# Set points for the side jobs of the scan, two operand buffers, and placed weight loads and stores

## The chip, the cores and the metric

The kernel runs on one core of a Trainium2 chip. The metric is the device time of one execution in microseconds (us); of several runs the median is taken. TensorE is called PE (its weight loads PEld), VectorE DVE, ScalarE ACT, GpSimd POOL. SP is the engine that issues nearly all DMAs here, one after the other.

## The reference

One step of a bidirectional diffusion backbone in fp32: 128 context and 1024 latent tokens of width 1024 go through SwiGLU FFN, token mixer, SwiGLU FFN, each between two RMS norms with modulation. The change is in the mixer:

```python
r, k, v, g, cb, cc, xc, gate_a, gate_b = split(h @ w_in)          # 5632 columns, 44 blocks of 128
kk = k * k_k; kk = kk * rsqrt(sum(kk * kk) + 1e-12)               # 8 heads of 64
for d in (forward, backward):
    decay = exp(-exp(w_log(xw)));  a = sigmoid(lora(xa));  k_d = k * (1 + (a - 1) * k_a)
    # per token: S = S * w + (S @ -kk) (kk * a)^T + v k_d^T ;  y = S @ r
    y_d, s_d = rwkv7_scan(r, decay, k_d, v, kk, a, s0[d], reverse=(d == 1))
y = groupnorm(y_0 + y_1) + bonus * v;  y_a = (y * sigmoid(g)) @ w_branch_a
y_b = (cb * conv3(cc * xc)) @ w_branch_b
out = (sigmoid(gate_a) * y_a + sigmoid(gate_b) * y_b) @ w_out
```

Latents start from a given state, the context from zero; the final context states are returned too.

## The kernel before

Activations lie transposed, 128 channels by tokens, the 1152 tokens in three tiles of 384. A product with a weight block is made of three matmuls for each 128 rows (high and low parts of fp32); `load_w` brings the weights (`wst`, two transfers of 256 KB for a column block), ACT rounds them to `whi` and POOL takes the rest as `wlo`. In the mixer each of the 44 column blocks of `w_in` is such a dense projection, `proj`: 24 triples, 72 matmuls into `pj`, evacuated by ACT to `fso` and stored to DRAM.

The scan works in chunks of 64 tokens, 18 items: 8 for each of two groups of heads (`g`), then 2 for the context. An item is a front for either direction (`stage_b`: load `ops` from DRAM, form decays, the products `scr`, the transposed operand `bkt`), a triangular solve on DVE (`solve`, its matmuls `l` and `l64b`), and two `step`s that carry the state (`sq`, `yp`). These make the chain. Three kinds of side jobs prepare and finish it: `stage_k` normalises k over heads (loads `or`, `ok`, `od`, `oi`; matmuls `cps`, `kkb`, `bon`; stores kk and the bonus `bvd`), `stage_v` transposes v, `finish` applies group norm and gate (`ysq`, `gv`) and stores `yad`. The rest of `proj` is filler, a generator (`stream`) of triples; `fill(40)` follows each item, and `need` fills on until a job that the chain waits for is written down.

What sets the order: a scheduler lists each engine's instructions by priority (chain 40000, side jobs 39000, filler least) and by its own idea of when an operand is ready; on the chip each engine then goes through its list in that order. A side job runs in a `Lane`: it yields a number of triples to wait between its steps, and its matmuls are put behind the filler triple that stands last (`PB.anchor`). Before the change the first projections (`job_rkv(1)`) are written ahead of the scan, the first four `stage_k` and those of item 0 as a whole without an anchor, weights are loaded as far ahead as three `wst` buffers let them, and every store is issued where its evacuation is written.

```python
        def fill(n):
            for _ in range(n):
                PB.anchor = next(filler, PB.anchor)
                clock["now"] += 1
                if clock["now"] - clock["side"] >= SG_ and any(lanes[x].tick() for x in "fkv"):
                    clock["side"] = clock["now"]
```

After the scan the two branches are read back (`brl`), split, and multiplied (`pb`, `pa`). What is left of the filler is run between.

## Time and profile before

| | us |
|---|---|
| median of 3 runs | 3284.18 (3278.63 to 3292.68) |
| profiled execution: device time, span of its instructions | 3273.45, 3271.7 |
| PE busy in it | 2994.4 (92%) |
| DVE, ACT, POOL busy | 1882.2, 1186.8, 394.7 |
| from the last product of the low-rank stage to the first `pb` | 1061.8 to 2190.4 |

How to read it: a row of the chain or the timeline has its start, its length and its name; what stands in brackets is the idle time of that engine just before it and what ended it. Engine, line and tile name an instruction (`PE cps L168`); two tiles with an arrow are what is written and what is read. PEclk is the share of the full TensorE clock, 2.4 GHz, that was granted; it has two levels, full and half.

### The profile page before, as it was taken

The numbers are of one execution on the slowest core, as the hardware profiler recorded it, in microseconds if no ns is written. First come the engines' busy times: TensorE is split into PE (matmuls) and PEld (weight loads), VectorE is DVE, ScalarE is ACT, GpSimd is POOL, SyncE is SP. The second block draws the span as 40 slices with busy tenths as digits, with TensorE's granted clock in tenths as the row PEclk, the third lists the DMA queues.
The fourth block names the chain that finished last, engine by engine and source line by source line (L and its number), as shares of the span: only waits on it lengthen the run. The fifth ranks groups of instructions, "written<-read, shape, count | busy, mean of one in ns | idle before, by whom it ended". The sixth has DMA issues, their size and how long they took to land.

```text
span 3271.7 us, 53390 instructions
## 1 busy us (share of the span) xinstructions
PE 2994.4 (92%) x20636; PEld 2816.4 (86%) x20636; DVE 1882.2 (58%) x4231; ACT 1186.8 (36%) x2726; POOL 394.7 (12%) x327
## 2 busy tenths in 40 slices
PE   8999999999989677787878888999989999999998
PEld 5999999999988565666767777799989999999998
DVE  7535665565872254677768889646683233323366
ACT  5521111114546242454445555332554211121244
POOL 1000000001250110122222222100130000000012
PEclk9999999999989787888889899999989999999999
DMA  8423333325544332322223332245532111111244
GB/s 270 145 62 96 97 103 86 88 83 154 160 123 163 101 100 65 107 74 88 71 63 98 101 93 84 86 153 158 170 103 84 39 44 45 43 40 42 81 145 132
DMA packets 470761, 330.67 MB, mean 101 GB/s; under 512 B 27424, under 2 KB 448620, under 8 KB 470508
## 3 DMA queue, kind: packets, MB, share of 16 engines
q1 hardware_dynamic: 469880, 326.78, 33.1%
q8 instruction: 162, 2.65, 0.3%
q14 instruction: 91, 0.75, 0.1%
q10 hardware_dynamic: 308, 0.44, 0.0%
q0 software_dynamic: 320, 0.04, 0.0%
HBM read 265.58 MB, written 61.60 MB: 100 GB/s over the span
## 4 chain that ended last, share of the span: by engine, by line
PE 40%; DVE 12%; DMA 8%; issue 4%; ACT 2%; SPq 1%; POOL 0%; DVEq 0%; ACTq 0%; POOLq 0%
PE po L211 3%; PE po L210 3%; PE po L212 3%; PE pg L212 3%; PE pg L211 3%; PE pg L210 3%; PE pu L210 3%; PE pu L212 3%; PE pu L211 3%; DMA oi<-opd 2%; PE pj L705 2%; PE pj L706 2%; PE pj L707 2%; DVE un L1031 2%; DMA opd<-oi 2%
## 5 line engine op out<-in xcount | busy, mean ns | idle before, releaser
L138 ACT ACTIVATE whi<-wst 128x512 fp32r<-128x512 f32 (+1 forms) x578 | 352.9, 612 | 771.2 <-PE po L212 391.5
L139 DVE TENSOR_TENSOR wlo<-wst,whi 128x512 fp32r<-128x512 f32 (+1 forms) x480 | 326.1, 680 | 314.2 <-ACT whi L138 304.2
L705 PE MATMUL pj<-hh,wlo 128*128 128x384 f32 x1056 | 390.1, 370 | 2.3 <-ACT fso L716 1.3
L706 PE MATMUL pj<-hl,whi 128*128 128x384 f32 x1056 | 389.1, 368 | 2.3 <-DVE hl L265 1.3
L707 PE MATMUL pj<-hh,whi 128*128 128x384 f32 x1056 | 387.4, 367 | 0.0
L211 PE MATMUL pg<-hl,whi 128*128 128x384 f32 x1056 | 356.4, 338 | 5.9 <-POOL hl L263 4.6
L210 PE MATMUL pg<-hh,wlo 128*128 128x384 f32 x1056 | 357.3, 338 | 1.3 <-DVE wlo L139 1.3
L210 PE MATMUL po<-ah,wlo 128*128 128x384 f32 x1056 | 354.8, 337 | 2.4 <-ACT ah L138 2.4
L212 PE MATMUL pg<-hh,whi 128*128 128x384 f32 x1056 | 355.5, 337 | 0.0
L210 PE MATMUL pu<-hh,wlo 128*128 128x384 f32 x1056 | 355.0, 336 | 0.0
L211 PE MATMUL po<-al,whi 128*128 128x384 f32 x1056 | 354.2, 336 | 0.4 <-DVE al L139 0.4
L211 PE MATMUL pu<-hl,whi 128*128 128x384 f32 x1056 | 354.0, 335 | 0.0
L212 PE MATMUL pu<-hh,whi 128*128 128x384 f32 x1056 | 353.8, 335 | 0.0
L212 PE MATMUL po<-ah,whi 128*128 128x384 f32 x1056 | 353.6, 335 | 0.0
L273 POOL TENSOR_TENSOR ss<-ss,sqt 128x384 f32<-128x384 f32 x78 | 89.3, 1148 | 1663.7 <-ACT sqt L272 1659.1
L426 DVE TENSOR_TENSOR sil<-sil,pu 128x384 f32<-128x384 f32 x132 | 72.8, 552 | 353.3 <-PE pu L212 353.3
L398 DVE TENSOR_TENSOR o<-o,po 128x384 f32<-128x384 f32 x288 | 159.1, 552 | 166.2 <-PE po L212 165.4
L706 PEld LDWEIGHTS pj<-hl,whi 128*128 128x128 f32 x1056 | 214.2, 203 | 11.3 <-DVE hl L265 2.1
L705 PEld LDWEIGHTS pj<-hh,wlo 128*128 128x128 f32 x1056 | 214.2, 203 | 11.1 <-issue 3.6
L707 PEld LDWEIGHTS pj<-hh,whi 128*128 128x128 f32 x1056 | 213.9, 203 | 8.1 <-issue 3.1
L211 PEld LDWEIGHTS pg<-hl,whi 128*128 128x128 f32 x1056 | 200.1, 190 | 8.4 <-POOL hl L263 6.2
L139 POOL TENSOR_TENSOR wlo<-wst,whi 128x512 fp32r<-128x512 f32 x98 | 134.1, 1372 | 594.5 <-ACT whi L138 459.5
(586 smaller groups left out, 5743.0 us busy)
## 6 DMA issues: line engine op xcount, KB each, us to landing
wst<-in_ffn_w SPq DMA_DIRECT2D x324, 256.0 KB
wmod<-in_w_mod SPq DMA_DIRECT2D x144, 256.0 KB
ops<-opd SPq DMA_DIRECT2D x36, 768.0 KB
wst<-in_w_in SPq DMA_DIRECT2D x94, 256.0 KB
wst<-in_ffn_w SPq DMA_DIRECT2D x96, 192.0 KB
xo<-xd SPq DMA_DIRECT2D x64, 192.0 KB
wst<-in_w_out SPq DMA_DIRECT2D x48, 256.0 KB
opd<-zv SPq DMA_DIRECT2D x24, 384.0 KB
```

The lines of the kernel that those rows point to most:

```text
L138: S.activation(out=hi, in_=src, func=AF.Copy)
L139: eng.tensor_tensor(out=lo, in0=src, in1=hi.bitcast(F32), op=ALU.subtract)
L210: PE.matmul(ps, lo, xh, start=(k == 0), stop=False)
L211: PE.matmul(ps, hi, xl, start=False, stop=False)
L212: later.tick(PE.matmul(ps, hi, xh, start=False, stop=(k == nk - 1)))
L273: eng.tensor_tensor(out=ssum, in0=ssum, in1=q, op=ALU.add)
L398: V.tensor_tensor(out=O[m][t], in0=O[m][t], in1=ps, op=ALU.add)
L426: V.tensor_tensor(out=s, in0=s, in1=pu, op=ALU.mult)
L705: PE.matmul(ps, lo, xh, start=(k == 0), stop=False)
L706: PE.matmul(ps, hi, xl, start=False, stop=False)
L707: ins = PE.matmul(ps, hi, xh, start=False, stop=(k == 7))
L1031: V.tensor_tensor(out=pv, in0=a, in1=b, op=ALU.mult)
```

## The change

- The first projections of heads 2 and 3 (`job_rkv(1)`) become part of the filler, which so grows from 38 to 41 column blocks. The first four `stage_k` and two `stage_v` calls become lane jobs ahead of item 0, with filler until they are done; those of item 0 become lane jobs too.
- A lane job's first instruction of a step, a load or an ACT or DVE operation, is also tied behind the filler triple (`first`), and the gaps grow: from the loads to the first operation 6 to 16 triples (now yielded ahead of the arithmetic), from norm to broadcast 6 to 14, in `finish` 3 to 6; between two steps of any job at least 2 triples, after each `stage_k` 8. The bonus comes last in `stage_k`, and the squares have a buffer of their own (`oa`).
- Weights of a projection are loaded behind the first triple of the one before (`plan`, `fetch`); a store is issued at the first triple that comes at least 6 after its evacuation (`late`, `stores`).
- `ops` has two buffers of five planes instead of one of six; the decay plane goes by two transfers of its own, in pieces of 256 bytes, into one of two `sg` tiles, and its scaling moves to the low-rank stage. `bk` is formed in place, so its transposition takes 8 matmuls of 64 rows instead of 4 of 128.
- Smaller scratch: `cent` has 64 columns, the widest product of the solve is made in two halves.

```diff
-    def load_w(src, nk, eng=V):
+    def load_w(src, nk, eng=V, behind=None):
...
+                dma = SP.dma_start(st[:, :n], src[k0 * 128:(k0 + n) * 128].rearrange("(k p) m -> p k m", p=128))
+                if behind is not None:
+                    after(dma, behind)
...
+        def first(self, ins):
+            self.put(ins)
...
-    cent = small("cent", 128)
-    V.scalar_tensor_tensor(out=cent, in0=bones, scalar=-1.0 / 64, in1=ident, op0=ALU.mult, op1=ALU.add)
+    cent = small("cent", 64)
+    for x in range(2):
+        hr = slice(64 * x, 64 * x + 64)
+        V.scalar_tensor_tensor(out=cent[hr], in0=bones[hr, hr], scalar=-1.0 / 64, in1=ident[hr, hr], op0=ALU.mult, op1=ALU.add)
...
+    late = deque()
+    def store(dst, src):
+        late.append((dst, src, clock["dense"]))
+    def stores(ins=None):
+        while late and (ins is None or late[0][2] + 6 <= clock["dense"]):
+            dst, src, _ = late.popleft()
+            dma = SP.dma_start(dst, src)
+            if ins is not None:
+                after(dma, ins)
+    clock = {"now": 0, "side": 0, "dense": 0}
+    plan, ahead = deque(), {}
+    def fetch(ins=None):
+        if plan:
+            col = plan.popleft()
+            ahead[col] = load_w(w_in[:, col:col + 128], 8, G, ins)
...
-        w = load_w(w_in[:, col:col + 128], 8, G)
+        if col not in ahead:
+            assert not plan or plan[0] == col
+            if plan:
+                fetch()
+            else:
+                ahead[col] = load_w(w_in[:, col:col + 128], 8, G)
+        w = ahead.pop(col)
...
+                clock["dense"] += 1
+                if k == 0 and t == ts[0]:
+                    fetch(ins)
+                stores(ins)
...
-            SP.dma_start(dst[:, t * TW:(t + 1) * TW], o)
+            store(dst[:, t * TW:(t + 1) * TW], o)
...
-        SG = st.tile([128, 4, 65], F32, name="sg")
+        SG = [st.tile([128, 4, 65], F32, name=f"sg{d}") for d in range(2)]
...
-        GI, GL, GM, GC, SG_ = 40, 6, 3, 6, 1
+        GI, GF, GL, GM, GC, SG_ = 40, 8, 16, 6, 14, 2
...
-                            o = out[0][:, pp] if i == 0 else q2.tile([128, 512], F32, name="lot", tag="bk")[:, :TW]
+                            o = e.tmp("lot")
                             S.activation(out=o, in_=ps2, func=AF.Tanh, scale=0.5, bias=(hw0, ha0)[i][:, d * 4 + p:d * 4 + p + 1])
-                            if i:
+                            if i == 0:
+                                V.tensor_scalar(out=out[0][:, pp], in0=o, scalar1=0.5, scalar2=0.5, op0=ALU.mult, op1=ALU.add)
...
+            k = q1.tile([128, 256], F32, name="ok", tag="ok")[:, :n]
+            PB.first(SP.dma_start(k, mirrored(p, 5, -1, t0, n)))
...
+            yield GL
+            a = q1.tile([128, 256], F32, name="oa", tag="oa")[:, :n]
+            PB.first(S.activation(out=a, in_=k, func=AF.Square, scale=e.KK_[:, p:p + 1]))
+            b = f0
+            PB.first(V.tensor_tensor(out=b, in0=f0, in1=f1, op=ALU.add))
...
+            yield 3
...
-            if not bon:
-                bonus()
+            yield 4
+            ps = ps_.tile([128, 256], F32, name="bon", tag="oc", bufs=1)[:, :n]
+            PB.matmul(ps, bones, b, start=True, stop=True)
+            o = v
+            V.tensor_tensor(out=o, in0=v, in1=ps, op=ALU.mult)
+            S.activation(out=o, in_=o, func=AF.Identity, bias=gb4[:, p:p + 1])
+            SP.dma_start(bvd[p][:, t0:t0 + n], o)
+            yield GF
...
-            ops = q1.tile([128, 6, 256], F32, name="ops", tag="ops")
-            SP.dma_start(ops.rearrange("p k (i t) -> p k i t", i=2), ops2[g][:, 3 * d:3 * d + 6, :, t0:t0 + 128])
-            td, X, r, kw = (ops[:, 0], ops[:, 1:3], ops[:, 3], ops[:, 4:6]) if d == 0 else (ops[:, 5], ops[:, 3:5], ops[:, 0], ops[:, 1:3])
+            ops = q2.tile([128, 5, 256], F32, name="ops", tag="ops")
+            sg = SG[d][:, :nb]
+            for pp in range(2):
+                SP.dma_start(sg[:, 2 * pp:2 * pp + 2, 1:65], ops2[g][:, 8 * d, pp, t0:t0 + 128].rearrange("p (s t) -> p s t", t=64))
+            SP.dma_start(ops.rearrange("p k (i t) -> p k i t", i=2), ops2[g][:, 1 + 2 * d:6 + 2 * d, :, t0:t0 + 128])
+            X, r, kw = (ops[:, 0:2], ops[:, 2], ops[:, 3:5]) if d == 0 else (ops[:, 3:5], ops[:, 0], ops[:, 1:3])
             c3 = "p (s t) -> p s t"
-            sg = SG[:, :nb]
-            S.activation(out=sg[:, :, 1:65], in_=td.rearrange(c3, t=64), func=AF.Copy, scale=0.5, bias=0.5)
...
-            BK = q2.tile([128, 4, 2, 64], F32, name="bk", tag="bk")[:, :nb]
-            c4 = "p x (s t) -> p s x t"
-            V.tensor_tensor(out=BK, in0=X.rearrange(c4, t=64), in1=kw.rearrange(c4, t=64), op=ALU.mult)
-            V.tensor_tensor(out=BK, in0=BK, in1=fb.unsqueeze(2).to_broadcast([128, nb, 2, 64]), op=ALU.mult)
+            BK = X
+            V.tensor_tensor(out=BK, in0=X, in1=kw, op=ALU.mult)
+            V.tensor_tensor(out=BK.rearrange("p x (s t) -> p x s t", t=64), in0=BK.rearrange("p x (s t) -> p x s t", t=64), in1=fb.unsqueeze(1).to_broadcast([128, 2, nb, 64]), op=ALU.mult)
...
-                PE.transpose(ps[:, i], BK[:, i].rearrange("p x t -> p (x t)"), ident)
+                for x in range(2):
+                    PE.matmul(ps[HR[x], i], BK[:, x, i * 64:i * 64 + 64], ident, start=True, stop=True)
...
-                dot(ap_(RR, 0, [(8, n), (1, 8)]), ap_(Lm, 32 * w, [(0, n), (32, 8), (1, w)]), ap_(YS, 0, [(32, n), (0, 8), (1, w)]), (n, 8, w))
+                for c in range(0, n, 3 if B == 3 else n):
+                    m = min(3, n) if B == 3 else n
+                    dot(ap_(RR, 8 * c, [(8, m), (1, 8)]), ap_(Lm, 32 * w, [(0, m), (32, 8), (1, w)]), ap_(YS, 32 * c, [(32, m), (0, 8), (1, w)]), (m, 8, w))
...
-        run(job_rkv(1))
...
-            for j in (job_rkv(2), job_rkv(3), job_g(0), job_g(1), job_conv(0), job_g(2), job_g(3), job_conv(1), job_conv(2), job_conv(3)):
+            for j in (job_rkv(1), job_rkv(2), job_rkv(3), job_g(0), job_g(1), job_conv(0), job_g(2), job_g(3), job_conv(1), job_conv(2), job_conv(3)):
...
+        for p in (1, 2, 3):
+            plan.extend((p * 128, 512 + p * 128, 1024 + p * 128))
+        cols_g, cols_c = ([1536 + p * 128] for p in range(4)), ([2048 + 512 + j * 128, 2048 + 1024 + j * 128, 2048 + j * 128] for j in range(4))
+        cols_g, cols_c = list(cols_g), list(cols_c)
+        for x in (cols_g[0], cols_g[1], cols_c[0], cols_g[2], cols_g[3], cols_c[1], cols_c[2], cols_c[3]):
+            plan.extend(x)
+        for m in range(8):
+            plan.extend((3584 + m * 128, 3584 + 1024 + m * 128))
...
+            return [("k", stage_k, 2 * g + pp, NCTX + b * 256, 256) for pp in range(2) for b in bs]
...
-        jobs = {1: ks(1, 0, 3), 4: ks(1, 1, 2), 5: fs(0, 1, 2) + vs(1, 0, 3), 7: fs(0, 0, 3) + vs(1, 1, 2), 10: kc(0) + kc(1),
+        jobs = {0: vs(0, 1, 2) + ks(0, 1, 2), 1: ks(1, 0, 3), 4: ks(1, 1, 2), 5: fs(0, 1, 2) + vs(1, 0, 3), 7: fs(0, 0, 3) + vs(1, 1, 2), 10: kc(0) + kc(1),
...
-        with beside():
-            for lane, f, *a in ks(0, 0, 3, bon=False) + vs(0, 0, 3):
-                run(f(*a))
+        side(ks(0, 0, 3) + vs(0, 0, 3))
+        need("kk", 0, 0, 3)
...
-            if i == 0:
-                with tc.high_priority(offset=39900):
-                    for lane, f, *a in vs(0, 1, 2) + ks(0, 1, 2, bon=False):
-                        run(f(*a))
```

The order of SP's instructions at the start of the scan, before (`L717`, `L730` store `fso`; `L151` loads weights; `L890`, `L892`, `L893`, `L946` load for `stage_k`, `L900` is its v, `L908` and `L922` its stores; `L958` loads `ops`):

```order
L151 DMA wst_11729<-in_w_in 128x4x128
L922 DMA opd0_110<-oi_10682 2x64x256
L890 DMA ok_10723<-opd0_110 128x1x256
L892 DMA od_10725<-opd0_110 128x1x256
L151 DMA wst_12142<-in_w_in 128x4x128
L958 DMA ops_10868<-opd0_110 128x12x128
L893 DMA oi_10726<-opd0_110 128x1x256
L730 DMA opd0_110<-fso_10534 2x64x384
L717 DMA vd1_113<-fso_10574 128x384
L900 DMA or_10677<-vd1_113 128x256
```

And in the change, with the same things on other lines (`L716` stores `fso`, `L932`, `L935`, `L936`, `L986` load, `L945` is v, `L964` and `L956` store):

```order
L956 DMA opd0_110<-oa_10491 2x64x256
L716 DMA opd0_110<-fso_10595 2x64x384
L935 DMA od_10659<-opd0_110 128x1x256
L964 DMA bvd0_116<-or_10404 128x256
L986 DMA or_10657<-opd0_110 128x256
L932 DMA ok_10655<-opd0_110 128x1x256
L716 DMA opd0_110<-fso_10633 2x64x384
L151 DMA wst_10675<-in_w_in 128x4x128
L151 DMA wst_10681<-in_w_in 128x4x128
L716 DMA opd0_110<-fso_10669 2x64x384
L716 DMA vd1_113<-fso_10709 128x384
L936 DMA oi_10905<-opd0_110 128x1x256
```

The two weight transfers of a projection stand together, between stores and the loads of one side job; `ok` still stands behind `or`, which has the buffer that the store `bvd` reads.

PE at the first context item, whose end states are transposed as `sf`, before:

```order
L705 MATMUL pj_21434<-hh2_0_8188,wlo_21424 128x384
L1125 MATMUL sq_20435<-zv0_9457,ab1_19694 64x64 x4
L1125 MATMUL sq_20435<-zv0_9457,ab0_19693 64x64 x4
L1126 MATMUL yp_20436<-ab0_19693,zv0_9457 64x64 x4
L1126 MATMUL yp_20436<-ab1_19694,zv0_9457 64x64 x4
L168 MATMUL cps_20043<-cst_81,ysq_20028 128x2 x2
L706 MATMUL pj_21434<-hl2_0_8189,whi_21423 128x384
L707 MATMUL pj_21434<-hh2_0_8188,whi_21423 128x384
L705 MATMUL pj_21434<-hh3_0_8219,wlo_21424 128x384
L706 MATMUL pj_21434<-hl3_0_8220,whi_21423 128x384
L707 MATMUL pj_21434<-hh3_0_8219,whi_21423 128x384
L1234 MATMUL sf_20497<-cst_81,ub0_9461 128x128
```

And in the change:

```order
L1167 MATMUL sq_21752<-zv0_9459,ab0_21093 64x64 x4
L1168 MATMUL yp_21753<-ab0_21093,zv0_9459 64x64 x4
L1168 MATMUL yp_21753<-ab1_21094,zv0_9459 64x64 x4
L1275 MATMUL sf_21814<-cst_81,ub0_9463 128x128
L1275 MATMUL sf_21820<-cst_81,ub1_9464 128x128
L1159 MATMUL yp_22002<-e0_21568,zv3_9462 64x64 x4
L1159 MATMUL yp_22002<-e1_21569,zv3_9462 64x64 x4
L177 MATMUL gv_21549<-cst_81,ysq_21511 128x128 x2
L174 MATMUL cps_21924<-cst_81,ysq_21561 128x2 x2
L177 MATMUL gv_21945<-cst_81,ysq_21561 128x128 x2
```

No filler stands there any more: in the order of the change the last of it comes early in the first context item, 21 matmuls behind the solve of that item.

## Rows read from the trace of the kernel before

**Rows 1.** Busy time by stretch: us, each engine busy (instructions), PEclk, DMA share, GB/s

```profile
1061.80:1211.50 149.70, 101.02 (x691) 92.43 (x689) 57.16 (x134) 43.29 (x100) 23.43 (x18) 0.82 0.35 105
1211.50:1260.00 48.50, 39.71 (x363) 30.87 (x362) 28.83 (x91) 18.88 (x58) 4.93 (x4) 0.79 0.18 56
1260.00:1375.50 115.50, 75.53 (x627) 64.71 (x626) 58.77 (x152) 40.15 (x108) 18.50 (x15) 0.81 0.33 99
1375.50:1663.40 287.90, 234.93 (x2470) 193.63 (x2470) 218.26 (x558) 141.96 (x398) 72.29 (x54) 0.87 0.26 78
1663.40:1791.30 127.90, 106.92 (x1066) 89.28 (x1066) 92.39 (x283) 61.64 (x174) 29.49 (x24) 0.90 0.28 82
1791.30:2045.10 253.80, 226.91 (x2488) 189.17 (x2490) 216.61 (x598) 140.53 (x405) 63.75 (x47) 0.91 0.31 91
2045.10:2190.40 145.30, 135.97 (x1103) 124.09 (x1103) 81.05 (x280) 53.10 (x135) 18.22 (x14) 0.99 0.36 113
1886.80:2045.10 158.30, 140.32 (x1641) 117.61 (x1643) 138.79 (x385) 90.21 (x260) 39.94 (x28) 0.95 0.30 89
2542.00:2624.00 82.00, 82.00 (x475) 82.00 (x475) 24.84 (x44) 16.89 (x32) 0.00 (x0) 1.00 0.14 42
```

**Rows 2.** The same stretches, the matmuls of the dense projections alone

```profile
1061.80:1211.50 149.70, 83.43 (x390) 0.82 0.35 105
1260.00:1375.50 115.50, 53.24 (x235) 0.81 0.33 99
1375.50:1663.40 287.90, 151.22 (x632) 0.87 0.26 78
1663.40:1791.30 127.90, 73.28 (x311) 0.90 0.28 82
1791.30:2045.10 253.80, 150.34 (x650) 0.91 0.31 91
2045.10:2190.40 145.30, 118.63 (x611) 0.99 0.36 113
1886.80:2045.10 158.30, 91.75 (x412) 0.95 0.30 89
```

**Rows 3.** Timeline of PE, a side job of the first ones: start, us, what

```profile
1145.99 1.01 PE L168 MATMUL cps<-cst,oi 128*128 128x2 f32 x4 [10.69 <-ACT oi L896]
```

**Rows 4.** Chain of what ended last, near 1260 us: start, us, what

```profile
1254.42 10.30 DMA bvd<-or
1265.11 5.67 DMA oi<-opd
```

**Rows 5.** Waits from 1060 to 2130 us: total us, times, longest

```profile
DVE od L895 <- DMA oi<-opd: 83.7, 15, 11.2
DVE bk L978 <- DMA ops<-opd: 64.1, 14, 16.8
```

**Rows 6.** Groups by line, whole span: the transposition of `bk`

```profile
L1004 PE MATMUL bkt<-cst,bk 128*128 128x128 f32 x144 | 26.4, 314 | 5.1 <-DVE ab L991 3.8 <-ACT e L994 1.1
```

**Rows 7.** DMA packets of the stretch 1886.8 to 2045.1 us

```profile
DMA packets 22728, 14.10 MB, mean 89 GB/s; under 512 B 820, under 2 KB 22708, under 8 KB 22708
```

**Rows 8.** Timeline of ACT, the squares of four finishing jobs

```profile
2081.45 0.42 ACT L1162 ACTIVATE ysq<-yl 128x256 f32<-128x256 f32 x1 [2.58 <-PE gv L171]
2086.25 0.42 ACT L1162 ACTIVATE ysq<-yl 128x256 f32<-128x256 f32 x1 [1.45 <-PE gv L171]
2107.59 0.31 ACT L1162 ACTIVATE ysq<-yc__20754 128x128 f32<-128x128 f32 x1
2116.05 0.31 ACT L1162 ACTIVATE ysq<-yc__21015 128x128 f32<-128x128 f32 x1 [2.10 <-DVE yc__21015 L1159]
```

**Rows 9.** Groups by line, 1060 to 2130 us: the split of the weights

```profile
L139 POOL TENSOR_TENSOR wlo<-wst,whi 128x512 fp32r<-128x512 f32 x72 | 96.6, 1345 | 523.4 <-ACT whi L138 389.6 <-issue 116.4 <-DVE nt L226 6.6
L138 ACT ACTIVATE whi<-wst 128x512 fp32r<-128x512 f32 x72 | 44.7, 627 | 46.1 <-PE pj L707 35.4 <-POOL wlo L139 6.5 <-issue 2.7
```

**Rows 10.** Waits of the DMA queue SP, the same stretch

```profile
SPq L151 <- POOL wlo L139: 173.0, 54, 10.0
```

More of the change, by code (lines that the diff above doesn't have):

```diff
@@ L1161, in finish @@
             a = q1.tile([128, 256], F32, name="ysq", tag="f4")[:, :n]
-            S.activation(out=a, in_=yo, func=AF.Square)
+            PB.first(S.activation(out=a, in_=yo, func=AF.Square))
             yield GM
@@ L1268, in front, with ks @@
                     stage_b(j, d, 0, A[i], i)
-        def ks(g, *bs, bon=True):
-            return [("k", stage_k, 2 * g + pp, NCTX + b * 256, 256, bon) for b in bs for pp in range(2)]
+        def ks(g, *bs):
+            return [("k", stage_k, 2 * g + pp, NCTX + b * 256, 256) for pp in range(2) for b in bs]
         def vs(g, *bs):
@@ L1317, in tick @@
                 return True
-        clock = {"now": 0, "side": 0}
         lanes = {x: Lane() for x in "fkv"}
```

59 lines of the change are left out of this document (22 added, 37 removed).

## The prediction

> **What bounds the kernel now.** I read the windows by stretch first [rows 1]. The change touches the scan, from the last low-rank product (1061.8) to the first `pb` (2190.4), 1128.6 us. In the first seven stretches PE is busy 820.99 of these, so it is idle for 207.6: 48.7, 8.8, 40.0, 53.0, 21.0, 26.9 and 9.3. The granted clock is 0.79 to 0.82 until 1375, 0.87 to 0.91 in the middle, 0.99 at the end. At full clock a matmul of a dense projection costs 82.00 / 475 = 0.173 us (the yardstick 2542 to 2624 [rows 1]); in the scan the same ones cost 83.43 / 390 = 0.214, 0.227, 0.239, 0.236 and 0.231, and 0.194 in the tail [rows 2]. So PE is the engine that carries the end, but it loses time twice: it waits, and it is paid at a lower clock behind the waits. Where products stand close (1886.8 to 2045.1), PE has 140.32 of 158.30.
>
> What it waits for: the timeline has PE stop 10.69 us ahead of a `cps` of a first side job, for `oi` of ACT [rows 3]; these matmuls stand in PE's list a few products behind the loads they need. The chain of waits goes back through `oi`, loaded in 5.67 us, to the store `bvd`, 10.30 us, which stands ahead of the next loads on SP [rows 4]. DVE waits 83.7 us in 15 places for `oi`, and 64.1 in 14 for `ops`, up to 16.8 each [rows 5]. All of these are latencies which products at the right place would cover.
>
> **The change, stretch by stretch.** The filler has 3 more column blocks, 216 products, that were paid ahead of item 0 before; the number of products in all stays. What changes is where they stand. By the order of before and after, counted between the solves (before in brackets; the matmuls of [rows 2], whose records can lack a few): ahead of the first solve 608 (390), then 80 (93), 462 up to item 3's (235), items 3 to 8 651 (632), items 9 and 10 454 (311), 11 to 16 620 (650), then 21 (611); 22 more stand ahead of the last low-rank product, 22 x 0.173 = 3.8 us. In `stage_k` 42 products now stand between `cps` and `kkb`, 12 to `bon`, and 81 to the next `cps`, 135 per job.
>
> Each stretch is built as products at full clock, plus the other work as it was, plus what idle time is left:
>
> - Up to the first solve: 608 x 0.173 = 105.2, other matmuls 101.02 - 83.43 = 17.6, and 15 for waits: `ok` still stands behind `or` on SP, which waits for `bvd` to land, so 10.30 + 5.67 [rows 4] and the arithmetic, some 16 to 19 us, stand against 81 x 0.173 = 14.0, up to 5 a job; I take three such jobs. 138 (before 149.7). Bounds: 0 and 35 (about what is idle and slow now).
> - Up to 1260: 48.5 - 13 x 0.173 = 46.
> - Up to 1375.5: 462 x 0.173 = 79.9, others 75.53 - 53.24 = 22.3, and half of the 40.0 idle, 20, since the solve's steps stay as they are. 122 (115.5).
> - Items 3 to 8: here the best that the trace shows is the yardstick 1886.8 to 2045.1, four items: 158.30 / 4 = 39.6 us for one. It holds 412 products, 103 an item, 17.8 us at 0.173, so 21.8 an item go to the rest. 6 x 21.8 + 651 x 0.173 = 243.4. `bkt` takes 8 matmuls for 4: one of 128 rows takes 26.4 / 144 = 0.18 us [rows 6]; I take 0.1 for one of 64, so 4 more an item and direction cost some 0.4 x 2, 5 us for six items (bounds 0, at half the price each, and 9 at the full 0.18). 248 (287.9). This is the largest gain, 40, and rests on the two `ops` buffers and the distances taking away the waits of [rows 5].
> - Items 9 and 10: 127.9 + 143 x 0.173 = 152.6, less half of what these waits are per item, (83.7 + 64.1) / 18 x 2 = 16.4, and the clock that comes back with them, together taken as 14.6. 138. Bounds: none of it, and twice it.
> - Items 11 to 16: as items 3 to 8, 6 x 21.8 + 620 x 0.173 + 5 = 243 (253.8).
> - The tail: filler runs out at the first context item. PE is left with 135.97 - 118.63 = 17.3 of other work and 21 products, 3.6. The lower end is DVE, 81.05 busy [rows 1]; the upper 145.3. Finishing jobs follow each other at 2086.25 - 2081.45 = 4.8 us, those of the context at 8.5 [rows 8]; eight of them in a row take 4 x 4.8 + 4 x 8.5 = 53, which fits under DVE's 81. I take 81.1 + 3.6 = 85, near the lower end, since PE, ACT and DMA all have slack there. Gain 60. The products that covered this stretch before now cover the waits earlier, which is the whole trade.
>
> Together 138 + 46 + 122 + 248 + 138 + 243 + 85 = 1020, + 3.8 - 1128.6 = **-105** us. Against the profiled execution of 3273.45 this gives 3168.7; the median of the runs is 3284.18, 10.7 above it, so 3179 as a median.
>
> Costed at nothing: the added scaling of decay in the low-rank stage lies under PE there, which has no wait for DVE in its rows; `sq` scratch and the smaller halves of the solve, a few instructions of an engine that waits less. The weights: POOL's part `wlo` takes 1.35 us and ACT's `whi` 0.63 [rows 9]. SP waited 173.0 us in 54 places for `wlo` [rows 10], with every load behind it in the queue; with a load placed behind the projection before, most of that goes, and I book no gain of its own.
>
> The decay planes go in pieces of 256 bytes, 512 packets a front, 1024 an item. In the stretch 1886.8 to 2045.1 there are 22728 packets [rows 7] at a DMA share of 0.30 [rows 1]: 16 x 158.3 x 0.30 / 22728 = 33 ns a packet, so 1024 / 16 x 0.033 = 2.1 us an item. The sum takes it as hidden, because the share of 0.30 leaves room and the loads go a buffer ahead; exposed in all 18 items it would be 38 us, 3217, inside the range. Only 820 of these 22728 packets are under 512 B [rows 7], so the trace hardly shows what a small one costs. The Trainium skill, page "DMA: Bandwidth & Descriptors", section "Specifications", says that transfers want at least 512 bytes to reach line rate; by that rule each of these packets would cost as one of twice its size, some 2 us more an item beside the loads they go with, and the sum would be the same while they are hidden.
>
> **The rivals.**
>
> A, the waits stay and each product that is moved ahead comes on top: loads and landings, not positions, set the pace. The stretches are then 187.4 + 46 + 154.8 + 291.2 + 152.6 + 248.6 + 85 = 1165.6 (each of before with its added products at 0.173), + 3.8 - 1128.6 = +41, **3325**, slower. For it speaks `ok` behind `or`; against it that PE's 10.69 us ended with `oi`, which has its load well ahead now, and that PE at 0.8 of the clock has more room. Half of it gives 3252.
>
> B, weights come late. They are loaded one projection ahead, a window of 72 x 0.173 = 12.5 us, less 0.63 and 1.35 for the split. It decides from a landing of 10.5 us: the longest in the rows is 10.30 [rows 4], and SP's mean wait for `wlo` was 173.0 / 54 = 3.2 us. If each of the 41 projections stood 3 us late, 123 us more: **3302**, slower. Against it: PE spends longer than 12.5 us on a projection in the scan, as other matmuls stand between.
>
> C, the dry tail is dearer or the waits go by a third only: 3252 to 3268. D, no idle time is left at all, `bkt` costs nothing and 9 and 10 gain twice: 3179 - 35 - 10 - 3.6 - 14.6 = 3116, and beyond. E, the positions in the list don't move the waits, and cover gained early is lost late: no change.
>
> **How the numbers follow.** A measurement can tell some 0.5% here, 16 us: faster is below 3268, slower above 3301. The forecast with its bounds, 3116 to 3252, has 0.70; C 0.08; times below D's 0.05; E, with A or B in part, 0.08; A in full 0.05, B 0.04. Faster is 0.70 + 0.08 + 0.05 = 0.83, the same 0.08, slower 0.09. The range runs from just under D, 3110, through C and a quarter of E, to 3275, and so holds 0.80.
>
> **What would show it.** Right: DVE's waits for `oi` and `ops` fall well below 83.7 and 64.1, PE has no 10 us gap ahead of `cps`, its clock stands above 0.9 from 1060 to the first context item, SP no longer waits for `wlo`, and a stretch of some 60 us with PE idle and at half clock stands ahead of `pb`. Wrong: gaps of PE ahead of `pj` that end with `wlo` or a weight load (B); items 3 to 8 still at 48 us (A); the tail at 120 us or more (C).

## The result

The change takes **3267.11 us** (median of 19 runs, 3256.87 to 3278.38) against 3287.03 us before (19 runs, 3278.48 to 3298.09): a ratio of 0.9936, 95% interval 0.9924 to 0.9948. It is faster, by 20 us (0.6%) and not by 105. The profiled execution of the change took 3270.18 us, 3.1 above its median; that of before, 3273.45, lies 13.6 under the median of its 19 runs. The two profiles therefore differ by 3.3 us only, and the tables below can place no more than that; the other 16 us lie between the profiles and their medians, 13.6 of them on the side of before, and have no stretch.

The windows of the change by the same stretches (columns as in [rows 1]; the last one is the first 109.60 us from the first `pb` on):

```profile
1059.50:1226.40 166.90, 138.59 (x882) 129.45 (x881) 58.00 (x147) 44.72 (x100) 31.00 (x24) 0.88 0.37 114
1226.40:1259.90 33.50, 32.71 (x374) 26.50 (x374) 24.20 (x75) 19.05 (x59) 5.71 (x4) 0.85 0.16 49
1259.90:1403.40 143.50, 123.94 (x946) 110.12 (x946) 71.86 (x183) 50.00 (x125) 33.46 (x26) 0.88 0.34 98
1403.40:1688.90 285.50, 246.93 (x2662) 201.15 (x2663) 231.20 (x607) 142.44 (x396) 75.82 (x59) 0.90 0.26 77
1688.90:1841.80 152.90, 132.53 (x1240) 115.05 (x1240) 95.30 (x283) 62.92 (x172) 27.32 (x21) 0.92 0.39 115
1841.80:2097.00 255.20, 233.68 (x2604) 190.50 (x2604) 213.43 (x599) 133.29 (x390) 53.96 (x40) 0.91 0.28 85
2097.00:2177.20 80.20, 40.89 (x500) 30.84 (x501) 50.61 (x215) 23.07 (x75) 0.00 (x0) 0.58 0.17 50
...
2177.20:2286.80 109.60, 106.54 (x584) 102.03 (x585) 74.23 (x151) 33.65 (x62) 0.00 (x0) 0.98 0.58 174
```

The same 109.60 us from the first `pb` on in the kernel before:

```profile
2190.40:2300.00 109.60, 109.60 (x634) 109.60 (x633) 64.97 (x117) 27.49 (x50) 0.00 (x0) 1.00 0.58 177
```

And the matmuls of the projections alone, as in [rows 2]:

```profile
1059.50:1226.40 166.90, 120.49 (x608) 111.25 (x606) 12.19 (x25) 0.88 0.37 114
1259.90:1403.40 143.50, 95.98 (x462) 84.01 (x462) 9.67 (x20) 0.88 0.34 98
1403.40:1688.90 285.50, 159.25 (x652) 121.41 (x651) 13.08 (x27) 0.90 0.26 77
1688.90:1841.80 152.90, 99.03 (x454) 82.04 (x454) 9.29 (x19) 0.92 0.39 115
1841.80:2097.00 255.20, 149.89 (x620) 113.80 (x620) 12.63 (x26) 0.91 0.28 85
```

| stretch | before | forecast | the change | products before, after |
|---|---|---|---|---|
| to the first solve | 149.7 | 138 | 166.9 | 390, 608 |
| to the second | 48.5 | 46 | 33.5 | 93, 80 |
| to that of item 3 | 115.5 | 122 | 143.5 | 235, 462 |
| items 3 to 8 | 287.9 | 248 | 285.5 | 632, 652 |
| items 9 and 10 | 127.9 | 138 | 152.9 | 311, 454 |
| items 11 to 16 | 253.8 | 243 | 255.2 | 650, 620 |
| tail, to the first `pb` | 145.3 | 85 | 80.2 | 611, 21 |
| from `pb` on | 1081.3 | 1081.3 | 1090.9 | none |

The scan starts 2.3 us earlier and takes 1117.7 us in place of 1128.6. From `pb` on 9.6 us are lost: the branches are split there and no longer beside filler, so PE runs 584 matmuls in the first 109.60 us and not 634, and 50 x 0.173 is 8.6 us.

The waits of the change from 1060 to 2130 us (total, times, longest), against [rows 5]:

```profile
ACT whi L138 <- DMA wst<-in_w_in: 84.7, 33, 17.2
DVE ops L1018 <- DMA ops<-opd: 43.3, 8, 10.1
DVE od L941 <- DMA od<-opd: 29.3, 5, 10.4
DVE od L942 <- DMA ok<-opd: 21.0, 3, 7.3
```

Two rows of before, of the same view, belong beside them:

```profile
DVE od L897 <- DMA ok<-opd: 20.5, 1, 20.5
ACT whi L138 <- DMA wst<-in_w_in: 0.8, 1, 0.8
```

And of the DMA queue SP, where [rows 10] had 173.0 us for `wlo`:

```profile
SPq L986 <- DMA bvd<-or: 45.4, 15, 6.3
```

DVE's waits for operands fell from 64.1 to 43.3 and those for the loads of `stage_k` from 104.2 (83.7 and 20.5) to 50.3. SP's waits for `wlo` are gone from among its longest. New are ACT's waits for weights, 84.7 us in place of 0.8. The waits that were forecast to go went; the time did not follow them.

### The profile page after: what moved, and what is told of

The parts are those of the page before. It is cut to its first block, busy times and chain, and to the rows that moved or that the text cites. A ratio compares the mean times of both kernels' runs of the same rounds, so it can differ in the third digit from the quotient of the medians.

```text
span 3268.1 us, 54468 instructions
## 1 busy us (share of the span) xinstructions
PE 3029.4 (93%) x21068; PEld 2839.3 (87%) x21068; DVE 1895.0 (58%) x4292; ACT 1175.7 (36%) x2690; POOL 389.5 (12%) x328
## 2 busy tenths in 40 slices
DMA packets 481135, 330.75 MB, mean 101 GB/s; under 512 B 47008, under 2 KB 458988, under 8 KB 480876
## 4 chain that ended last, share of the span: by engine, by line
PE 43%; DVE 14%; DMA 4%; ACT 2%; issue 2%; SPq 0%; POOL 0%; DVEq 0%; ACTq 0%; POOLq 0%
PE po L217 3%; PE po L216 3%; PE po L218 3%; DVE un L1071 3%; PE pg L218 3%; PE pg L217 3%; PE pg L216 3%; PE pu L216 3%; PE pu L217 3%; PE pu L218 3%; PE pj L741 3%; PE pj L742 3%; PE pj L740 3%; DMA opd<-oa 1%; DVE tb L1072 1%
## 5 line engine op out<-in xcount | busy, mean ns | idle before, releaser
L216 PEld LDWEIGHTS po<-ah,wlo 128*128 128x128 f32 x1056 | 198.7, 188 | 3.9 <-ACT ah L138 3.9
```

Of the source, the lines that this page charges most:

```text
L216: PE.matmul(ps, lo, xh, start=(k == 0), stop=False)
```

## What sets the pace of an item

**Fewer and more products.** In the first pair each triple of the projections loses a matmul or gets a fourth.

```diff
-                PE.matmul(ps, lo, xh, start=(k == 0), stop=False)
-                PE.matmul(ps, hi, xl, start=False, stop=False)
+                PE.matmul(ps, hi, xl, start=(k == 0), stop=False)
```

> Of the changed kernel, every triple of a dense projection loses its first matmul (the product with wlo), so 1056 matmuls are left out and y is less exact; nothing else is changed. Theory C (from the second item on an item lasts as long as the chain of the scan on DVE and its hand-overs; products beside it have no price there): items 3 to 8 (285.5 us in the changed kernel, 217 matmuls fewer) and 11 to 16 (255.2, 207 fewer) stay within 10 us each, and the time comes only from the stretches that are filled on purpose: 203 fewer up to the first solve, 153 up to item 3's, 151 in items 9 and 10, at most 507 x 0.173 = 88 us less; total 3170 to 3230. Theory P (PE sets the pace and each product costs its time wherever it stands): 1056 x 0.173 = 183 us less, 3085, with items 3 to 8 some 38 us and items 11 to 16 some 36 us shorter.

> The counterpart: every triple of a dense projection gets a fourth matmul (the product with wlo twice, so y changes in its low part), 1056 more. Theory C: an item of 3 to 8 then has 13 + 141 x 0.173 = 37 us of PE work in 47, so items 3 to 8 and 11 to 16 grow by under 12 us each; the stretches filled on purpose grow by their products, 507 x 0.173 = 88 us; total 3355 to 3385. Theory P: 183 us more, 3450. A third theory (the half clock behind idle PE makes the chain slow): items 3 to 8 get shorter, since PE is idle less, by up to the 32 us that the clock costs there.

Measured: 3231.38 us with a third out (ratio to before 0.9837, 0.9802 to 0.9873), 36 under the change and 1 over the range of theory C; 3423.86 with a fourth in (1.0423, 1.0386 to 1.0461), 157 above the change and between the theories. Items 3 to 8 and 11 to 16 with a third out:

```profile
1379.20:1671.00 291.80, 249.85 (x2702) 205.43 (x2702) 239.19 (x616) 153.59 (x420) 94.83 (x70) 0.89 0.33 98
1809.20:2057.00 247.80, 155.31 (x2098) 123.54 (x2097) 197.89 (x561) 119.09 (x358) 37.00 (x28) 0.67 0.22 63
```

The matmuls of the projections alone in these two stretches:

```profile
1379.20:1671.00 291.80, 161.41 (x674) 124.66 (x674) 20.93 (x43) 0.89 0.33 98
1809.20:2057.00 247.80, 35.87 (x123) 24.94 (x123) 3.90 (x8) 0.67 0.22 63
```

The scheduler refilled items 3 to 8 (674 products), so these say nothing. But the filler then ran dry in items 11 to 16: 123 products and not 620, PE busy 155.31 in place of 233.68, its clock at 0.67, and the stretch got only 7.4 us shorter. By the forecast's price 497 products are 86 us. **Products taken from beside items 11 to 16 give back next to nothing.** That the half clock costs nothing there is not shown: DVE had 15.5 us less to do (197.89 in place of 213.43), so its waits grew by 8 us, and the median `sq` matmul of the chain (those of `zv` and `e`) took 314 ns in place of 222.

The stretches that are filled on purpose lost 494 products (up to the first solve, items 1 and 2, items 9 and 10) and only 37 us: 0.05 to 0.11 us each, where theory C allowed 0.173. A product can cost its full time there (0.165 us in `rkv_ahead` below), but need not.

The fourth matmul fell between the two theories: 315 of its products went to items 9 and 10 (769 there, 211.2 us, 58 more), and the tail has 316 and not 21. It does not show that products can be added for nothing either. Items 3 to 8 have 58 more and take 13 us more. The chain's own waits on DVE, sorted as in the table below, rise from 39 to 68 us there, and in items 11 to 16 from 31 to 52, with 33 products fewer; there 18 us less side work hides it. No run shows whether the longer triples or the order did that.

**Double work on DVE.**

```diff
                 V.tensor_tensor(out=pv, in0=a, in1=b, op=ALU.mult)
+                V.tensor_tensor(out=pv, in0=a, in1=b, op=ALU.mult)
```

> Every multiplication of the triangular solve on DVE is made twice (same values, same result): 14 instructions, 8.7 us more per solve by their mean lengths in the changed kernel, 157 us in 18 solves. Theory C: each item grows by nearly that, 7 to 9 us, items 3 to 8 from 285.5 to 330 to 338, items 11 to 16 from 255.2 to 300 to 308; total 3390 to 3425. Theory P: DVE is busy some 39 of 47 us in an item, so most of the 8.7 us fits beside PE: under 3 us an item, total 3267 to 3310.

Measured: 3405.36 us (1.0363, 1.0325 to 1.0401), 138 above the change and in the range of the theory of the chain on DVE, though both stretches are longer than it said (366.5 in place of 330 to 338, 309.1 in place of 300 to 308). Its items 3 to 8 and 11 to 16:

```profile
1419.20:1785.70 366.50, 312.68 (x2940) 262.12 (x2941) 283.43 (x723) 153.17 (x418) 90.95 (x68) 0.83 0.25 75
1926.20:2235.30 309.10, 225.62 (x2457) 183.82 (x2457) 246.90 (x678) 129.18 (x378) 46.48 (x34) 0.74 0.23 68
```

And the matmuls of the projections alone:

```profile
1419.20:1785.70 366.50, 215.28 (x884) 171.76 (x884) 18.00 (x37) 0.83 0.25 75
1926.20:2235.30 309.10, 117.70 (x472) 90.93 (x472) 9.77 (x20) 0.74 0.23 68
```

DVE's busy time grew by 52 and 33 us, the stretches by 81 and 54. None of it fitted beside PE. Why more than itself was paid is open: DVE's waits grew along (from 54 to 83 us, and from 42 to 62), but the first stretch also has 233 products more than in the change, and in the second, with 148 fewer, PE's clock fell from 0.91 to 0.74.

**Where the forecast's 40 us in items 3 to 8 went.** I sorted DVE's instructions there by the function of their line: the chain (`solve`, its products, `stage_b`, `step`) and the side jobs with the evacuations of the filler; each idle time is counted to the instruction that ended it. The four terms make the length (us, worked out from the trace):

| items 3 to 8 | length | chain | side | waits, chain | waits, side (for DMA) |
|---|---|---|---|---|---|
| before | 287.9 | 187.0 | 31.2 | 38.6 | 31.0 (26.0) |
| the change | 285.4 | 186.0 | 45.1 | 39.4 | 14.9 (7.2) |
| old distances | 306.8 | 179.8 | 51.2 | 39.0 | 36.7 (18.0) |
| middle distances | 302.3 | 177.4 | 52.6 | 41.3 | 31.1 (16.7) |
| middle, then full | 269.5 | 185.1 | 38.2 | 37.9 | 5.6 (0.9) |
| one operand buffer | 266.2 | 182.6 | 41.9 | 37.4 | 4.3 (0.0) |
| less side work | 249.8 | 184.5 | 21.3 | 37.1 | 6.9 (0.0) |
| weights as before | 268.5 | 180.8 | 40.9 | 34.9 | 11.2 (0.0) |
| products ahead | 265.9 | 185.5 | 37.9 | 33.5 | 8.9 (0.0) |

The change took 16 us of waits of the side jobs out of these items, and 14 us of their work came in; the chain's own waits stayed. The last two rows are `fetch_now` and `rkv_ahead` (below), which leave the chain and the side jobs as they are written. With other loads or other filler beside them the same items are 17 to 20 us shorter, so a difference of that size between two rows proves no cause by itself.

The groups of DVE in items 3 to 8 show which work came in. Before (count, busy us, mean ns):

```profile
L227 DVE SCALAR_TENSOR_TENSOR ny<-nt,ny 128x4 f32<-128x4 f32 x18 | 3.9, 214 | 0.1
L792 DVE SCALAR_TENSOR_TENSOR cnv<-ccs,cw,cnv 128x378 f32<-128x378 f32 (+2 forms) x8 | 4.5, 566 | 0.0
```

The same groups in the change: 8 reciprocal roots of three steps in place of 6, and more taps of the convolution, that is another piece of filler.

```profile
L233 DVE SCALAR_TENSOR_TENSOR ny<-nt,ny 128x4 f32<-128x4 f32 x24 | 5.1, 218 | 0.2
L834 DVE SCALAR_TENSOR_TENSOR cnv<-ccs,cw,cnv 128x378 f32<-128x378 f32 (+2 forms) x11 | 6.2, 566 | 0.0
```

**Less side work**, the test of that reading:

```diff
-        for _ in range(3):
+        for _ in range(it):
...
-        return rsq(ps, n * nr, scale, eps)
+        return rsq(ps, n * nr, scale, eps, 1 if tag == "oc" else 3)
...
-                    V.scalar_tensor_tensor(out=cc[:, :, 1:], in0=uu[:, :, :w_ - 1], scalar=cw2[:, j:j + 1], in1=cc[:, :, 1:], op0=ALU.mult, op1=ALU.add)
...
```

> The change with less work of side jobs on DVE: the two side taps of the convolution (scalar_tensor_tensor into cnv) and two of the three Newton steps of the side jobs' reciprocal roots are left out, so the result is less exact and y_b wrong. In items 3 to 8 of the change these are 12.6 us of the taps and 8 x 6 x 0.24 = 11.5 us of the steps. Theory D (DVE goes through its list in order, chain and side jobs together, and an item lasts as long as DVE's work and waits): items 3 to 8 get 15 to 24 us shorter, 285 to 262 to 270, the whole 30 to 60 us faster, 3207 to 3237. Rival (side jobs fit in the pauses of the chain on DVE): items 3 to 8 within 6 us, total 3255 to 3268.

Measured: 3231.17 us (0.9832, 0.9813 to 0.9851), 36 under the change; items 3 to 8:

```profile
1399.80:1649.60 249.80, 226.84 (x2608) 185.17 (x2608) 205.78 (x538) 140.48 (x390) 75.96 (x58) 0.93 0.29 85
```

249.8 us, 36 less, where 15 to 24 were expected: 24 of work and 8 of waits with it. Part of that can be such a move. Against the four kernels of the table that take 266 to 270 us, it has 17 to 21 us less side work and is 16 to 20 us shorter, one for one. The side jobs don't fit into the pauses of the chain; they stand in its list. Items 11 to 16 got only 2.5 shorter (252.7) although 9 us of side work went: there the chain's own waits rose from 31 to 41, so the reading is shown for items 3 to 8 and not for these.

## What each part is worth

**The distances**, as one line with other numbers (here `mid_gaps`; `old_gaps` has those of before, and `split_gaps` a second line that sets the full ones once the second item is written):

```diff
-        GI, GF, GL, GM, GC, SG_ = 40, 8, 16, 6, 14, 2
+        GI, GF, GL, GM, GC, SG_ = 40, 2, 10, 4, 10, 2
```

> The distances of the side jobs lie between the old and the new ones (GF 2, GL 10, GM 4, GC 10, SG_ 2 for 8, 16, 6, 14, 2). By the order 476 products stand ahead of the first solve (608 in the change, 390 before), 500 behind the last (21 and 611). Theory C: the products that leave the start, items 1 and 2 and items 9 and 10 (465) save up to 0.15 us each there, and in the tail the first 200 lie in PE's idle time and also keep the clock for pb; the rest is paid: 10 to 20 us less than the change, 3247 to 3257. Theory P: products only move, within 8 us of the change, 3260 to 3275.

> The change with the distances of the kernel before (GF 0, GL 6, GM 3, GC 6, SG_ 1), all else as in the change. By the order 420 products stand ahead of the first solve, 551 behind the last. If the distances carry the gain of the change (each wait of a side job covered by products), it is lost: 3280 to 3295. Theory C (products put ahead of the first solve, into items 1 and 2 and 9 and 10 are paid in full, those beside items 3 to 16 are free): the distances are what costs, and without them the time is below the change, as in mid_gaps: 3238 to 3258, the start near 145 us, the tail near 130.

> The middle distances of mid_gaps until the second item is written, the full ones of the change from then on. In mid_gaps items 3 to 8 took 302.3 us against 285.4 in the change, with the same products (652, 651) and PE idle 51.5 against 38.5. If this is the price of the small distances (side jobs on DVE and ACT that wait for their loads and hold up the chain), items 3 to 8 come back to some 285 and the time falls below mid_gaps, to 3225 to 3240. By the order 404 products stand in items 9 and 10 (315 in mid_gaps), which costs some of it. Rival: the 17 us come from how the scheduler happened to order the chain; then items 3 to 8 stay at some 300 and the time is 3242 to 3256.

| distances | us | ratio to before | start | items 1, 2 | 3 to 8 | 9, 10 | 11 to 16 | tail |
|---|---|---|---|---|---|---|---|---|
| old | 3272.72 | 0.9965 (0.9947 to 0.9983) | 142.6 | 130.4 | 306.8 | 127.6 | 256.8 | 136.5 |
| middle | 3244.62 | 0.9876 (0.9832 to 0.9919) | 144.4 | 126.0 | 302.3 | 118.6 | 252.4 | 124.4 |
| middle, then full | 3241.66 | 0.9853 (0.9820 to 0.9886) | 146.7 | 125.0 | 269.5 | 158.4 | 256.5 | 104.6 |
| full (the change) | 3267.11 | 0.9936 (0.9924 to 0.9948) | 166.9 | 143.5 | 285.4 | 152.9 | 255.2 | 80.2 |

The middle distances came out a little under what theory C gave (3247 to 3257). Neither theory had the old distances right: 3272.72 lies between them, 5.6 us over the change. The stretches say where. Going from old to full, items 3 to 8 gain 21, and the tail 56; the start pays 24, items 1 and 2 13, items 9 and 10 25, and `pb` 8.5. The full distances keep the side jobs' waits off DVE in items 3 to 8, and they are paid in products wherever the chain has to wait until a job is written down (`need`). The middle ones cost the start nothing against the old (144.4, 142.6), and the tail still has 500 products, which keep PE at 117.40 of 124.40 us, and nothing is lost behind it (1082.1 us from `pb` on, 1081.3 before):

```profile
2036.20:2160.60 124.40, 117.40 (x980) 107.01 (x981) 70.68 (x256) 49.78 (x129) 15.47 (x12) 0.96 0.39 118
```

Full distances from the second item on bring items 3 to 8 down by 33, where 17 were expected, but items 9 and 10 get 89 more products and take 40 more: the time is that of the middle ones, and between the two expectations.

**Products ahead of the first solve.**

```diff
+        run(job_rkv(1))
         items = [(g, j) for g in range(2) for j in range(8)] + [(2, 0), (2, 1)]
...
-            for j in (job_rkv(1), job_rkv(2), job_rkv(3), ...
+            for j in (job_rkv(2), job_rkv(3), ...
```

> The change with the first projections of heads 2 and 3 again ahead of the scan and not in the filler. By the order 822 products stand ahead of the first solve (608 in the change), and the filler runs dry in the last items, 7 between the solves of items 15 and 16. Theory C: the 214 more cost 37 us at the start, less what they still cover of its 28 us of idle time, and the last items lose nothing by having no products: 3285 to 3304. Theory P: the same products in all, the same time, 3260 to 3275; by a third view (the half clock) the last items without products get longer by some us each, 3310 and more.

Measured: 3305.37 us (1.0071, 1.0050 to 1.0093), 38 above the change, 1 over the range of theory C. The stretch up to the first solve, and items 11 to 16:

```profile
1058.50:1260.70 202.20, 174.60 (x1111) 165.28 (x1109) 59.88 (x149) 53.29 (x116) 38.69 (x30) 0.92 0.34 104
1873.10:2132.50 259.40, 208.83 (x2411) 168.59 (x2411) 206.83 (x597) 128.00 (x378) 46.99 (x34) 0.81 0.26 76
```

214 more products ahead of the first solve cost 35 us, 0.165 each: they cover nothing there that isn't covered yet. Items 11 to 16 have 427 in place of 620 and are 4 us longer, not shorter, with 6.6 us less work on DVE and PE's clock at 0.81: here too a price of the half clock is not ruled out. So this part of the change, taken alone, is worth 38 us: it takes products from a place where they are paid. The larger distances put nearly as many back (608 there, 420 with the old ones).

**The second operand buffer** (the same in the low-rank stage, which borrows it):

```diff
-            ops = q2.tile([128, 5, 256], F32, name="ops", tag="ops")
+            ops = q2.tile([128, 5, 256], F32, name="ops", tag="ops", bufs=1)
```

> The change with one operand buffer in place of two (also in the low-rank stage, which borrows it, so that this stage is read apart). Theory C (the chain on DVE sets the pace): the load of a front can start only when the one before has been read, so its landing comes onto DVE; DVE waited 64.1 us in 14 places for ops in the kernel before, 43.3 in 8 in the change; in the scan 20 to 60 us more, total 3285 to 3330. Rival: the fronts are formed early enough and the wait is beside the chain, then within 8 us of the change.

Measured: 3253.73 us (0.9894, 0.9864 to 0.9925), 13 **under** the change, outside both expectations, although its scan starts 11 us later. Items 3 to 8 and 11 to 16 are 19 and 16 us shorter:

```profile
1409.40:1675.50 266.10, 234.68 (x2630) 190.78 (x2629) 224.45 (x606) 140.43 (x389) 75.64 (x57) 0.91 0.28 81
1836.60:2075.70 239.10, 220.16 (x2571) 178.13 (x2570) 205.51 (x592) 133.68 (x388) 55.33 (x40) 0.94 0.32 95
```

The second buffer brings nothing here. Why one is better is not settled. DVE's side work and waits are 14 us less in items 3 to 8, but this is no more than `fetch_now` and `rkv_ahead` bring there without touching it. With the middle distances one buffer again makes these items 19 us shorter (283.4 in `mid_one` below, 302.3), though this time by the chain's waits (26.3 in place of 41.3): seen twice, by different terms, and no run shows that the buffer itself did it.

**Weights and the queue.** `fetch_now` undoes the placed loads, `bon_oi` takes the store `bvd` out of the way of `or`:

```diff
-        w = ahead.pop(col)
+        w = load_w(w_in[:, col:col + 128], 8, G)
...
-                if k == 0 and t == ts[0]:
-                    fetch(ins)
```

```diff
-            SP.dma_start(f1, mirrored(p, 7, -1, t0, n))
-            yield GL
+            yield 8
+            PB.first(SP.dma_start(f1, mirrored(p, 7, -1, t0, n)))
+            yield GL - 8
...
-            o = v
+            o = f1
```

> The change with the weights of a projection loaded as before the change, as far ahead as the three buffers let them, in place of behind the first triple of the projection before. SP then waits for POOL again ahead of a weight load (173.0 us in 54 places before). Theory C: that holds up the loads of side jobs, which costs only up to item 2 and in items 9 and 10; but weights can't be late there as in the first job: 3258 to 3280, no clear difference. If the placed loads carry the gain of the change: 3280 to 3290, back at the kernel before.

> The change, but the bonus of a side job is written into the buffer of oi, which the next job loads last, 8 triples into its distance, in place of that of or. In the change SP waits 45.4 us in 15 places ahead of the load of or for the store bvd to land, and the weights stand behind it: in the first job they landed 17.2 us after ACT wanted them, the evacuation fso stood behind on ACT, and PE stopped 11.3 us. If that is the cause, this stop goes and with it up to 16 us of the stretch up to the first solve (166.9); the total falls by 8 to 20 us, 3247 to 3259. From item 3 on the chain sets the pace and nothing is gained. Rival: the weights are late by themselves (one projection ahead is too little); then ACT still waits over 10 us for wst there and the time stays at 3262 to 3270.

> split_gaps with the bonus in the buffer of oi (bon_oi). bon_oi alone took 10 us off the change, 7 of them up to the first solve, by freeing SP ahead of the weights. In split_gaps 476 products stand there and the longest wait of ACT for weights was 7.9 us. If the two add up: 3241.7 - 10 = 3232, range 3225 to 3238; if the distances already leave SP enough time, 3238 to 3248.

Measured: 3263.26 us (0.9930, 0.9908 to 0.9953), 3257.51 (0.9907, 0.9878 to 0.9936) and 3262.20 (0.9938, 0.9918 to 0.9957). The placed loads make no difference that the runs can tell. What `bon_oi` was about stands in the timeline of the change: SP issues the store, waits until it has landed, and the weights come behind; ACT waits for them with an evacuation behind, and PE stops for that evacuation. First SP (start, us, what):

```profile
1072.43 3.08 SPq L964 DMA_DIRECT2D bvd<-or  x1
1081.94 0.33 SPq L986 DMA_DIRECT2D or<-opd  x1
...
1083.55 4.24 SPq L151 DMA_DIRECT2D wst<-in_w_in  x2
```

Then ACT, with the idle time ahead in brackets:

```profile
1093.74 0.63 ACT L138 ACTIVATE whi<-wst 128x512 fp32r<-128x512 f32 x1 [17.20 <-DMA wst<-in_w_in]
...
1095.07 0.47 ACT L755 ACTIVATE fso<-pj 128x384 f32<-128x384 f32 x1
```

And PE:

```profile
1095.59 0.69 PE L740 MATMUL pj<-hh,wlo 128*128 128x384 f32 x1 [11.26 <-ACT fso L755]
```

With the store in another buffer PE still stops there, for 6.7 us in place of 11.3, and ACT still waits 12.62 us, the rival's sign: 4.6 us of the stop came with the store. The stretch went from 166.9 to 159.5. The rest came with the placed loads: in `fetch_now`, with the store as in the change, neither ACT's waits for weights nor this stop are there, SP waits 145.7 us for `wlo` again, and the stretch takes 161.6 us.

With the middle distances it doesn't add up: `split_bon` is 20 us slower than `split_gaps`, outside both expectations. Items 3 to 8 take 285.8 us in place of 269.5 and items 11 to 16 265.9 in place of 256.5. The load of `oi` now stands late in the job, and DVE waits for it 64.3 us in 8 places, up to 21.9; but in `split_gaps` it waits 65.7 us for the other loads of `stage_k`, so this does not explain the difference, and its cause is open.

**Towards the fastest version.**

> The middle distances of mid_gaps and one operand buffer (ops_one) together, as the candidate for the fastest. ops_one alone was 13 us under the change though its low-rank stage was 11 us longer, and its items 3 to 16 were shorter. If that comes from the single buffer itself, the two add up: 3244.6 - 13 = 3232, range 3224 to 3240. If it is only another order of the same work, 3240 to 3255 and items 3 to 16 as long as in mid_gaps (673 us).

> mid_one with the weights loaded as before the change, as far ahead as the buffers let them. In the change itself this made no clear difference (3263 against 3267). The same here: 3214 to 3232. If SP's waits for POOL ahead of a weight load hold up the loads of side jobs, which stand at smaller distances here: 3232 to 3250.

> mid_one (3222 us) with the Newton steps of the side jobs on POOL in place of DVE, 15 small POOL instructions for 9 of DVE, same result up to rounding. Some 9 x 0.24 = 2.2 us of DVE work leave it for each of 36 jobs, 78 us. Theory D: the part of it in the items counts, some 20 to 35 us: 3187 to 3205. Rival: the longer way over POOL (each job waits for it) holds up the next instruction of the side job on DVE, and with it the chain: 3222 to 3260.

Measured: `mid_one`, middle distances and one operand buffer, 3222.29 us (0.9816, 0.9789 to 0.9843), just under the range for two gains that add up; with the weights loaded as before the change 3224.74 (0.9814, 0.9788 to 0.9840), the same. This is the fastest, 45 us under the change. On POOL the steps made it 3277.67 (0.9977, 0.9961 to 0.9993): the rival's case, and worse than it. The edit is

```diff
-            V.tensor_tensor(out=tt, in0=y, in1=y, op=ALU.mult)
+            G.tensor_tensor(out=tt, in0=y, in1=y, op=ALU.mult)
```

and so on, with DVE then waiting for the result ahead of the side jobs' next instructions and of everything behind them:

```profile
DVE oa L963 <- POOL ny L252: 53.3, 18, 6.5
...
DVE ysq L1221 <- POOL ny L252: 42.4, 15, 5.5
```

95.7 us of waits came for some 78 of work. The 55 us by which it is slower than `mid_one` do not lie in items 3 to 8 (284.7 us, 283.4 there) but in items 11 to 16 (22 more) and in the tail (35 more, with 586 products in place of 486), so how much of them is the hand-over and how much are products that moved stays open.

## Why the prediction was right and wrong

The direction was right, and 3267.11 lies in the range of 3110 to 3275, but in the part above 3252 that was kept for the rivals; the size was wrong by a factor of five. Point by point:

- **What bounds the kernel**: wrong for items 3 to 16. I read PE as the engine that carries the end, since it was busy most and lost time to waits and clock. What the runs move these items by is DVE's list, chain and side jobs together. It stood in [rows 1]: DVE has 138.79 of 158.30 us in the yardstick, 0.88, PE 140.32 with a clock of 0.95, and I had taken only PE's column. PE's idle time in items 11 to 16 was slack; for its half clock that is not shown. (In that paragraph PE's busy time is summed wrongly: the seven stretches have 920.99 us, not 820.99. The idle time of 207.6 is right.)
- **Items 3 to 8** (248, measured 285.5), the mis-sized term with the most in it. The step that failed is the yardstick (21.8 us an item beside the products), which took DVE's part to be the same in all items. Sorted as in the table, its four items have 15.9 us of side work, 14.2 of waits of the chain and 5.2 of the side jobs; for six that is 24, 21 and 8, and the change has 45.1, 39.4 and 14.9. So 21 us more are side work and 18 are waits of the chain, which stayed at 38 to 41 us with all distances; of the 39.4, 22.0 end with ACT, 7.5 with PE and 5.6 with DMAs. The side jobs' waits went (16 us), and 14 us of side work took their place. The second `ops` buffer, on which the gain was to rest, brought none (266.2 without it). That some 248 can be reached is shown by the run with less side work, 249.8. **Items 11 to 16** (243, measured 255.2): the same step, with 31.4 us of side work and 31.3 of waits of the chain.
- **Up to the first solve** (138, measured 166.9): here products do have a price, and I took 0.173 for each where the clock stayed at 0.88: 120.49 / 608 = 0.198, 15 us more; and idle time was 28.3 in place of 15. The stop of 11.26 us is rival B, as a single event: the weights landed late. ACT waited for weights 33 times, but only here with a stop of PE over 2 us behind it. I had SP's order in front of me and took the store `bvd` to hold up `ok` only, not the weights behind it.
- **To the solve of item 3** (122, measured 143.5): the idle time was right (19.6, forecast 20). 462 products cost 0.208 each, 16 us more than at 0.173, and other matmuls 28.0 and not 22.3. **Items 9 and 10** (138, measured 152.9): what rival A gave, 152.6, with PE idle for 20.4 us as before (21.0). The stretch **to the second solve** (46, measured 33.5) was better than forecast: it is 30 to 36 us in all kernels in which item 0's side jobs are lane jobs, except the one with double work on DVE (53.4).
- **The tail** (85, measured 80.2): the number was right by luck. The stretch did run dry, with PE idle for 39 us and its clock at 0.58, but its floor was not DVE's 81.05 us of work: DVE is busy for 50.61 and waits for the rest. 18 of the 81 us were splits of the branches, which now stand behind the first `pb`. The dry stretch has a sequel that I had at nothing: 9.6 us from there on. The 3.8 us ahead of the scan didn't show; it starts 2.3 us earlier.
- **Rival A** was given 0.05 in full; in the stretches that are filled on purpose it is what happened. The trade I described, cover moved from the tail to the waits, was there, but with products at 0.165 to 0.21 us in a place where most of the waits were not PE's to lose. That price is not fixed: in `third_out` the same stretches gave back 0.05 to 0.11 us a product.
- **The 256-byte pieces**: the Trainium skill, page "DMA: Bandwidth & Descriptors", section "Specifications", wants at least 512 bytes a transfer for line rate. The packets under 512 B rose from 27424 to 47008 in the whole run, and the DMA share of items 3 to 8 stayed at 0.26. None of the longest 200 groups of waits in the change ends with a load of `sg`. No run took these transfers apart, so none shows the price of that rule here.
- Of what I named as signs, the waits for operands and `stage_k` and SP's for `wlo` fell, the gap ahead of `cps` went, the idle tail came; the clock did not stay above 0.9 (0.85 to 0.92). Of the signs of being wrong two came: B's stop ahead of `pj`, once, and A's items 3 to 8 at 48 us (285.5 / 6 = 47.6).

Open remains where 16 of the 20 us lie that the medians show and the two profiles don't, why one operand buffer is faster than two, what lengthens the chain's waits where the matmuls change, and how much of the 45 us of `mid_one` is a luckier order.

## What to carry to other kernels

Before a wait is counted as a gain, ask on whose list the stretch ends: add up that engine's work and waits in one stretch (chain, side work, waits of either), and see whether they make its length. That sum always comes out, so it shows a bound only together with a run that adds or takes work of one of its terms. Filler is worth its cover where the chain waits, and can cost up to its full price where the chain has to wait until so much of it is done. Beside a chain on another engine, taking it away gained next to nothing here. An edit also reorders everything the scheduler lists: look how far a stretch moves under edits that should not touch it before a difference there is given a cause. A yardstick taken from another stretch holds only if the limiting engine has the same work there.

## What was not expected of the hardware

- PE at half clock for much of six items (0.67 granted, 155.31 us busy of 247.80) left them at 247.8 us, against 255.2 at 0.91, with 15.5 us less work on DVE and 8 us more waits.
- DVE work that was added to the solve, 52 us of busy time in items 3 to 8, came with a stretch 81 us longer: the waits around it grew too (side jobs' 14.9 to 29.8, the chain's 39.4 to 53.3), with 233 products more beside it.
- 15 small POOL instructions of 0.22 to 0.26 us in place of 9 of DVE for each of the side jobs' roots: DVE waited 95.7 us for their results, for some 78 us of work taken off it.
